# Splitting the gated retention output where it is formed, and loading both parts straight into the operand tiles

## The chip, the cores and the metric

The kernel runs on one core of one Trainium2 chip. The metric is the device time of one execution in microseconds (us). All values are float32. Products are made to full accuracy out of three matmuls on "split" operands: a tile x is kept as a high part hi (x rounded to the shorter type fp32r) and a low part lo = x - hi, and a product w*x is formed as hi*hi + hi*lo + lo*hi. So every matmul operand has to be split once, by a cast on ScalarE (ACT) and a subtraction on VectorE (DVE). TensorE is PE here, GpSimd is POOL, and SP is the SyncE queue that issues most of the DMAs.

## The reference, cut to what matters

One layer of a streaming encoder on 1024 prompt tokens and 64 sample tokens (T = 1088 columns in the kernel), model width 1024. The part around the change:

```python
def merge_branches(ret_o, ret_g, swa_o, gate_a, gate_b, w_ret_out, w_swa_out, w_mix_out):
    B, S = ret_g.shape[:2]
    a = (rms_norm(ret_o).astype(ret_g.dtype).reshape(B, S, -1) * jax.nn.silu(ret_g)) @ w_ret_out
    b = swa_o.reshape(B, S, -1) @ w_swa_out
    return (jax.nn.sigmoid(gate_a) * a + jax.nn.sigmoid(gate_b) * b) @ w_mix_out
```

`ret_o` is the output of multi-scale retention, normalised per head; `ret_g`, `gate_a` and `gate_b` are column blocks of one projection of the normalised input; `swa_o` is the output of sliding-window attention. After this come cross attention to 256 memory tokens, a SwiGLU and a last norm.

## The kernel before, in words

Activations are kept transposed: 128 partitions of model dimension by T columns, so a 1024-wide activation is KT = 8 tiles. The work is staged:

- `project_phase` (to about 825 us): projections with Strassen's seven products on halves of 544 columns (`strassen`, `weight_ops`), with retention of the four heads in between. Its operands B11, B21, B22, T1 to T4 lie in two rings of SBUF tiles: `rings[0]` and `rings[1]`, eight slots each, a slot being [128, 2, T]. Retention's normalised output goes to DRAM as `d_ret`.
- The last three projections of that phase are the gates: `w_ga` (sigmoid), `w_rg` (silu) and `w_gb` (sigmoid), each in four pairs of 128 output rows, each pair in two halves of columns. `project` evacuates a result into a `stage` tile (DVE), multiplies it by the token norm (DVE), applies the activation (ACT), and for `w_rg` alone loads `other` (the tile of `d_ret`, four buffers), multiplies on POOL, and stores the product to `d_gate[0]`. Between them steps of `memory_phase` run (`w_mk`, half of `w_mv`).
- `mix_phase` (from about 825 us): sliding-window attention (`swa`), 34 half-steps of scores, softmax, transpose and weighting (`scores`, `turn`, `weigh`). Between the half-steps PE does pieces of other products, handed out by `filler`: first the other half of `w_mv`, in eight pieces ahead of the first transposes, and then `w_ret_out` on the gated retention output, in 48 half-pieces of 12 matmuls. `in_order` fixes the order of PE's work here.
- `filler` first brings the gated retention output back: `operands(c0, n)` loads, for each of eight tiles and one of three chunks of columns CH (384, 384, 320), a part of `d_gate[0]` into a small tile `ld()` (ten of them, cut out of two slots of ring 0, named swin in the profile), and splits it (`split`: ACT at L123, DVE at L124) into `rets`, the eight slots of ring 1 (named ret in the profile).
- `merge_swa` and the later phases follow; the change does not touch them.

All queues are static: a scheduler that simulates the program's time line orders each engine's instructions when the kernel is built. `tc.issue_after(x)` keeps an instruction from being ordered before x; `high_priority` puts it early. SP's DMAs are issued in that fixed order: an issue that has to wait for a buffer holds up all behind it. `unit_raw` loads a slab of weights into one of two `raw` buffers; `unit_parts` splits it into `wq` tiles.

Of the kernel before, what the change touches and what calls it, by code (L numbers as in the profile page):

```python
# [11 lines left out]
F32 = mybir.dt.float32  # L12
F32R = mybir.dt.float32r
# [6 lines left out]
P = 128  # L20
D = 1024
KT = D // P
SEQ = 1024
SMP = 64
T = SEQ + SMP
CH = ((0, 384), (384, 384), (768, 320))
# [83 lines left out]
class Kernel:  # L110
# [8 lines left out]
    def store(self, out, in_):  # L119
        self.nc.sync.dma_start(out, in_)  # L120
# [212 lines left out]
    def run(self):  # L333
        nc, tc, io = self.nc, self.tc, self.io
        with ExitStack() as ctx:
            cp = ctx.enter_context(tc.tile_pool(name="const", bufs=1, reuse_waits="tile"))
            self.np = ctx.enter_context(tc.tile_pool(name="norm", bufs=1, reuse_waits="tile"))
            dp = ctx.enter_context(tc.tile_pool(name="scratch", bufs=1, reuse_waits="tile", space=DRAM))

            self.ident = cp.tile([P, P], F32, name="ident")  # L340
            self.ones = cp.tile([P, P], F32, name="ones")
            self.gains = cp.tile([P, 5, KT], F32, name="gains")
            self.load(self.gains, io["g_all"])
            nc.vector.memset(self.ones, 1.0)
            self.rstd = cp.tile([P, T], F32, name="rstd")

            self.root = cp.tile([P, len(CH), 3], F32, name="root")
            self.rtok = cp.tile([P, 9], F32, name="rtok")
            nc.vector.memset(self.rtok, 1.0)
            self.mtok = cp.tile([P, 2], F32, name="mtok")  # L350
            self.tab = cp.tile([P, 2, H, 3], F32, name="tab")
            self.tok = cp.tile([P, 3, H, 9], F32, name="tok")
            self.sinks = cp.tile([P, NPAIR], F32, name="sinks")

            self.d_mk = dp.tile([H, P, 2, NMEM], F32, name="d_mk")
            self.d_mv = dp.tile([H, P, 2, NMEM], F32, name="d_mv")
            self.d_ret = dp.tile([KT, P, T], F32, name="d_ret")
            self.d_swa = dp.tile([KT, P, T], F32, name="d_swa")
            self.d_gate = [dp.tile([KT, P, T], F32, name=f"d_gate{i}") for i in range(3)]
            self.d_mix = dp.tile([KT, P, T], F32, name="d_mix")  # L360
            self.d_h = [dp.tile([KT, P, T], F32, name=f"d_h{i}") for i in range(2)]
            self.d_op = dp.tile([len(OPS), FT // 2, P, HALF], F32, name="d_op")
            self.d_rb = dp.tile([16, 64 * 256], F32, name="d_rb")

            self.d_qkv = dp.tile([3, KT, P, T], F32, name="d_qkv")
            self.d_skv = dp.tile([2, P, T], F32, name="d_skv")
            self.d_sq = dp.tile([NPAIR // 2, P, 17, 2, 64], F32, name="d_sq")

            with ExitStack() as sctx:
                self.rings = [Ring(sctx.enter_context(tc.tile_pool(name=f"ring{i}", bufs=1, reuse_waits="tile", side="right")))  # L370
                              for i in range(2)]
                self.mem = sctx.enter_context(ExitStack())
                with self.weights(5):
                    self.project_phase()
                with self.weights(6):
                    with self.plain_psum():
                        self.mix_phase()
                        self.mem.close()
                        self.cross_phase()
                    rp = sctx.enter_context(tc.tile_pool(name="rf", bufs=1, reuse_waits="tile", side="right"))  # L380
                    self.rstd_f = rp.tile([P, T], F32, name="rstd_f")
                    self.temp = sctx.enter_context(ExitStack())
                    self.new_b12(self.temp, side="right")
                    self.cross_out_phase()
                    self.ffn_phase()
# [153 lines left out]
    def project_phase(self):  # L539
        nc, tc, io = self.nc, self.tc, self.io  # L540
        with ExitStack() as ctx:
# [9 lines left out]
            half = lambda t: slice(t * HALF, (t + 1) * HALF)  # L551
# [11 lines left out]
            def project(w, put, act=None, other=None):  # L563
                def emit(i, t, ps, sb):
                    o = taken(ps, sb)
                    (nc.vector if act is not None else nc.gpsimd).tensor_tensor(
                        out=o, in0=o, in1=self.rstd[:, half(t)], op=ALU.mult)
                    if act is not None:
                        nc.scalar.activation(o, o, act)
                    if other is not None:  # L570
                        r = op.tile([P, HALF], F32, tag="other", bufs=4, name="other")
                        self.load(r, other(i)[:, half(t)])
                        nc.gpsimd.tensor_tensor(out=o, in0=o, in1=r, op=ALU.mult)
                    put(i, t, o)
                cast = self.last_cast
                self.strassen(w, self.ops, emit)
                return cast
# [71 lines left out]
            steps = [0, 0, 0, 0, 1, 2, 2, 2, 3, 3, 2, 0]  # L649
            for idx, w, act in ((1, "w_ga", AF.Sigmoid), (0, "w_rg", AF.Silu), (2, "w_gb", AF.Sigmoid)):  # L650
                for m in range(0, KT, 2):
                    store = nc.scalar.dma_start if idx else self.store
                    put = lambda i, t, o, idx=idx, m=m, store=store: store(self.d_gate[idx][m + i, :, half(t)], o)
                    other = None if idx else lambda i, m=m: self.d_ret[m + i]
                    with tc.issue_after(project(pair(w, m // 2), put, act, other)):
                        for i in range(steps.pop(0)):
                            if (idx, m, i) == (0, 6, 0):
                                with tc.issue_after(self.last_mm):
                                    next(memory)
                            else:  # L660
                                next(memory)
# [378 lines left out]
    def filler(self):  # L1040

        nc, tc, io = self.nc, self.tc, self.io
        if True:
            def ld():
                self.lds.append(self.lds.pop(0))
                return self.lds[-1]

            rets = self.ring_tiles(1, KT, "ret")

            def operands(c0, n):  # L1050
                after = self.loaded
                for k in range(KT):
                    a = ld()
                    with tc.issue_after(after):
                        ins = self.load(a[:, :n], self.d_gate[0][k, :, c0:c0 + n])
                    if c0 == 0:
                        self.operand_loaded = ins
                    self.split(a[:, :n], rets[k][:, 0, c0:c0 + n], rets[k][:, 1, c0:c0 + n])

            raws = [self.unit_raw(io["w_mv"][3, i], 4, 256) for i in range(2)]  # L1060
            operands(*CH[0])
            for h in range(2, H):
                us = self.first_units if h == 2 else [self.unit_parts(raw, 4, 256) for raw in raws]
                operands(*CH[h - 1])
                for t in range(2):
                    ps = self.dense_psum()
                    for k in range(KT):
                        x = self.ms[k][:, :, t * P:(t + 1) * P]
                        self.mm3(ps[:, :256], x[:, 0], x[:, 1], *us[k // 4][k % 4], k == 0, k == KT - 1)
                        if k == 3:  # L1070
                            yield
                    o = ld()[:, :256]
                    nc.scalar.mul(o, ps[:, :256], self.mtok[:, t:t + 1])
                    self.store(self.d_mv[h, :, t, :], o)
                    self.store(io["o_mv"][t * P:(t + 1) * P, h * 256:(h + 1) * 256], o)
                    yield
            for m in range(KT):
                u = self.unit(io["w_ret_out"][m], KT)
                for c0, n in CH:
                    g = ld()  # L1080
                    self.load(g[:, :n], self.d_gate[1][m, :, c0:c0 + n])
                    for ps in self.pieces(u, rets, c0, n):
                        if ps is None:
                            yield
                    nc.vector.tensor_tensor(out=g[:, :n], in0=ps, in1=g[:, :n], op=ALU.mult)
                    self.store(self.d_mix[m, :, c0:c0 + n], g[:, :n])
                    yield
# [512 lines left out]
```

## Time and profile before

| | us |
|---|---|
| median of 3 runs | 2273.01 (2269.17 to 2275.49) |
| the profiled execution | 2270.68 |
| its span, first to last instruction | 2268.9 |
| mean granted PE clock over the span | 0.983 |

The profile is of one execution. Each engine's busy time counts its instructions alone, not its waits; "PEld" is the weight load that overlaps the matmuls. A wait is given as the waiting instruction, then the one that released it. In the DMA issues, "KB" is the size of one transfer and the last number the median us from issue to landing. DMA share is the mean busy share of the core's 16 DMA engines.

### The profile page before, as it was taken

The page shows a single profiled execution, that of the slowest core. Times are in us where ns is not written, and L with a number is a line of the kernel's source. Part 1 is how long each engine was busy: PE and PEld are TensorE (multiplying, and loading weights), DVE is VectorE, ACT ScalarE, POOL GpSimd, SP SyncE. Part 2 cuts the span into 40 slices and gives each one's busy share as a digit, 9 for nine tenths or more (in the row PEclk, how much of TensorE's full clock was granted, in tenths as well). Part 3 has the DMA queues.
Part 4 walks back from the last instruction along what each step waited for, and adds up shares of the span by engine and source line. Part 5 has one row for each costly group of instructions (what it writes and reads, how often), then busy time and mean ns, then how long its engine had stood idle before and what let it go on. Part 6 is the DMA issues. An engine that isn't in the chain of part 4 may idle for free.

```text
span 2268.9 us, 41687 instructions
## 1 busy us (share of the span) xinstructions
PE 2187.2 (96%) x16382; PEld 2121.9 (94%) x16382; DVE 1594.4 (70%) x2656; ACT 895.8 (39%) x1921; POOL 692.5 (31%) x466
## 2 busy tenths in 40 slices
PE   7999999999999989999999999999999999999996
PEld 7999998999999987778999998999999999999996
DVE  8986877666687658875455555676676776878596
ACT  7333333345444355553133333333222222344344
POOL 1441533332243112220000000014555555434471
PEclk9999999999999999999999999999999999999997
DMA  5644445443454475326443112422333332475223
GB/s 191 190 139 132 131 146 140 132 134 117 150 164 154 146 241 174 113 70 196 141 151 106 56 48 67 133 81 88 116 128 103 101 118 90 143 266 194 79 90 107
DMA packets 186406, 298.64 MB, mean 132 GB/s; under 512 B 40514, under 2 KB 111074, under 8 KB 186210
## 3 DMA queue, kind: packets, MB, share of 16 engines
q1 hardware_dynamic: 181602, 287.06, 39.6%
q10 hardware_dynamic: 4608, 8.91, 1.1%
q8 instruction: 129, 2.11, 0.4%
q14 instruction: 67, 0.55, 0.1%
HBM read 204.75 MB, written 91.16 MB: 130 GB/s over the span
## 4 chain that ended last, share of the span: by engine, by line
PE 77%; DVE 12%; DMA 5%; issue 3%; ACT 2%; POOL 1%; SPq 0%; DVEq 0%; ACTq 0%; POOLq 0%
PE pq L205 14%; PE pq L208 14%; PE pq L206 14%; PE pd L149 7%; PE pd L150 7%; PE pd L151 7%; DVE wq L124 2%; PE pout L987 2%; PE pp L971 1%; PE pss L929 1%; DMA cs<-c_rope 1%; DVE B L124 1%; DMA hl<-d_op 1%; DVE T L124 1%; DVE stage L560 1%
## 5 line engine op out<-in xcount | busy, mean ns | idle before, releaser
L123 ACT CAST wq<-raw 128x512 fp32r<-128x512 f32 (+1 forms) x509 | 310.2, 614 | 567.6 <-PE pq L208 275.9
L124 DVE TENSOR_TENSOR wq<-raw,wq 128x512 fp32r<-128x512 f32 (+1 forms) x509 | 449.6, 887 | 119.7 <-ACT wq L123 117.5
L205 PE MATMUL pq<-T,wq 128*128 128x272 f32 x1832 | 502.5, 292 | 2.9 <-DVE T L124 2.4
L206 PE MATMUL pq<-T,wq 128*128 128x272 f32 x1832 | 498.8, 289 | 0.0
L205 PE MATMUL pq<-B,wq 128*128 128x272 f32 x1592 | 439.2, 293 | 11.3 <-ACT wq L123 10.1
L206 PE MATMUL pq<-B,wq 128*128 128x272 f32 x1592 | 437.2, 291 | 7.7 <-DVE B L124 7.6
L208 PE MATMUL pq<-T,wq 128*128 128x272 f32 x1832 | 383.7, 289 | 0.6 <-DVE wq L124 0.6
L183 POOL TENSOR_TENSOR raw<-raw 128x512 f32<-128x512 f32 (+1 forms) x59 | 83.1, 1408 | 892.4 <-DVE wq L124 663.1
L205 PEld LDWEIGHTS pq<-T,wq 128*128 128x128 f32 x1832 | 346.7, 189 | 3.8 <-ACT wq L123 3.2
L206 PEld LDWEIGHTS pq<-T,wq 128*128 128x128 f32 x1832 | 349.9, 191 | 0.3 <-issue 0.3
L208 PE MATMUL pq<-B,wq 128*128 128x272 f32 x1592 | 334.3, 290 | 0.0
L206 PEld LDWEIGHTS pq<-B,wq 128*128 128x128 f32 x1592 | 305.9, 192 | 10.1 <-DVE B L124 9.7
L205 PEld LDWEIGHTS pq<-B,wq 128*128 128x128 f32 x1592 | 303.1, 191 | 11.9 <-ACT wq L123 10.1
L208 PEld LDWEIGHTS pq<-T,wq 128*128 128x128 f32 x1832 | 286.3, 189 | 1.9 <-DVE wq L124 1.2
L208 PEld LDWEIGHTS pq<-B,wq 128*128 128x128 f32 x1592 | 250.4, 190 | 0.5 <-issue 0.3
L252 DVE TENSOR_TENSOR u<-pq,u 128x544 f32<-128x544 f32 x177 | 127.5, 720 | 120.5 <-PE pq L208 119.8
L186 POOL TENSOR_TENSOR raw<-raw 128x512 f32<-128x512 f32 (+1 forms) x59 | 83.7, 1419 | 122.7 <-DVE wq L124 115.1
L957 POOL TENSOR_TENSOR t<-t,den 128x768 f32<-128x768 f32 (+2 forms) x34 | 47.9, 1408 | 173.5 <-DVE den L955 87.7
L560 DVE TENSOR_TENSOR stage<-pq,u 128x544 f32<-128x544 f32 x112 | 80.2, 716 | 28.5 <-PE pq L208 28.4
L184 POOL TENSOR_TENSOR raw<-raw 128x512 f32<-128x512 f32 (+1 forms) x59 | 87.1, 1476 | 3.7
L189 POOL TENSOR_TENSOR raw<-raw 128x512 f32<-128x512 f32 (+1 forms) x59 | 83.7, 1419 | 4.5
L1434 POOL TENSOR_TENSOR y<-u,y 128x544 f32<-128x544 f32 x38 | 62.5, 1652 | 73.7 <-DVE y L1432 51.5
(356 smaller groups left out, 4685.5 us busy)
## 6 DMA issues: line engine op xcount, KB each, us to landing
hl<-d_op SPq DMA_DIRECT2D x85, 272.0 KB, 4.4
d_qkv<-stage SPq DMA_DIRECT2D x44, 272.0 KB, 4.4
d_op<-stage SPq DMA_DIRECT2D x44, 272.0 KB, 2.2
d_op<-ht SPq DMA_DIRECT2D x44, 272.0 KB, 3.2
raw<-w_gate SPq DMA_DIRECT2D x22, 512.0 KB, 3.4
raw<-w_up SPq DMA_DIRECT2D x22, 512.0 KB, 4.8
cs<-c_rope SPq DMA_DIRECT2D x16, 544.0 KB, 4.3
d_gate<-stage ACTq DMA_DIRECT2D x32, 272.0 KB, 2.4
```

The source lines that it names most:

```text
L123: self.last_cast = self.nc.scalar.copy(hi, src).ins
L124: self.nc.vector.tensor_tensor(out=lo, in0=src, in1=hi.bitcast(F32), op=ALU.subtract)
L149: mm(ps, wh, xh, start=start, stop=False)
L150: mm(ps, wh, xl, start=False, stop=False)
L151: self.last_mm = mm(ps, wl, xh, start=False, stop=stop).ins
L184: tt(out=a21, in0=a21, in1=a22, op=add)
L186: tt(out=a11, in0=a22, in1=a11, op=sub)
L205: mm(ps[:, c, :HC], w[:, 0, ks], x[:, 0, cs], start=start, stop=False)
L206: mm(ps[:, c, :HC], w[:, 0, ks], x[:, 1, cs], start=False, stop=False)
L208: self.last_mm = mm(ps[:, c, :HC], w[:, 1, ks], x[:, 0, c * HC:(c + 1) * HC], start=False, stop=stop).ins
L252: add = lambda out, a, b: nc.vector.tensor_tensor(out=out, in0=a, in1=b, op=ALU.add)
L560: nc.vector.tensor_tensor(out=o, in0=ps, in1=sb, op=ALU.add)
```

## The change

The product of `w_rg`'s projection and `d_ret` is split at once: the cast writes the high part over the `other` tile, the subtraction leaves the low part in the `stage` tile. Both go to DRAM, into a new tensor `d_gret` [KT, 128, 2, T], by two stores in place of one. `operands` in `filler` has no splits and no small tiles any more: it loads both parts of a chunk with one DMA into the slot of ring 1, in the order 0, 1, 4, 5, 6, 7, 2, 3, the first chunk not before the memory weights loaded ahead (`after`), the later ones not before the first chunk's last load.

```diff
@@ -356,7 +356,8 @@
             self.d_mv = dp.tile([H, P, 2, NMEM], F32, name="d_mv")
             self.d_ret = dp.tile([KT, P, T], F32, name="d_ret")
             self.d_swa = dp.tile([KT, P, T], F32, name="d_swa")
-            self.d_gate = [dp.tile([KT, P, T], F32, name=f"d_gate{i}") for i in range(3)]
+            self.d_gate = [None] + [dp.tile([KT, P, T], F32, name=f"d_gate{i}") for i in (1, 2)]
+            self.d_gret = dp.tile([KT, P, 2, T], F32, name="d_gret")
             self.d_mix = dp.tile([KT, P, T], F32, name="d_mix")
             self.d_h = [dp.tile([KT, P, T], F32, name=f"d_h{i}") for i in range(2)]
             self.d_op = dp.tile([len(OPS), FT // 2, P, HALF], F32, name="d_op")
@@ -571,7 +572,12 @@
                         r = op.tile([P, HALF], F32, tag="other", bufs=4, name="other")
                         self.load(r, other(i)[:, half(t)])
                         nc.gpsimd.tensor_tensor(out=o, in0=o, in1=r, op=ALU.mult)
-                    put(i, t, o)
+                        hi, lo = r.bitcast(F32R), o.bitcast(F32R)
+                        self.split(o, hi, lo)
+                        put(i, t, 0, r)
+                        put(i, t, 1, o)
+                    else:
+                        put(i, t, o)
                 cast = self.last_cast
                 self.strassen(w, self.ops, emit)
                 return cast
@@ -649,8 +655,10 @@
             steps = [0, 0, 0, 0, 1, 2, 2, 2, 3, 3, 2, 0]
             for idx, w, act in ((1, "w_ga", AF.Sigmoid), (0, "w_rg", AF.Silu), (2, "w_gb", AF.Sigmoid)):
                 for m in range(0, KT, 2):
-                    store = nc.scalar.dma_start if idx else self.store
-                    put = lambda i, t, o, idx=idx, m=m, store=store: store(self.d_gate[idx][m + i, :, half(t)], o)
+                    if idx:
+                        put = lambda i, t, o, idx=idx, m=m: nc.scalar.dma_start(self.d_gate[idx][m + i, :, half(t)], o)
+                    else:
+                        put = lambda i, t, part, o, m=m: self.store(self.d_gret[m + i, :, part, half(t)], o)
                     other = None if idx else lambda i, m=m: self.d_ret[m + i]
                     with tc.issue_after(project(pair(w, m // 2), put, act, other)):
                         for i in range(steps.pop(0)):
@@ -1047,21 +1055,18 @@
 
             rets = self.ring_tiles(1, KT, "ret")
 
-            def operands(c0, n):
-                after = self.loaded
-                for k in range(KT):
-                    a = ld()
+            def operands(c0, n, after):
+                for k in (0, 1, 4, 5, 6, 7, 2, 3):
                     with tc.issue_after(after):
-                        ins = self.load(a[:, :n], self.d_gate[0][k, :, c0:c0 + n])
-                    if c0 == 0:
-                        self.operand_loaded = ins
-                    self.split(a[:, :n], rets[k][:, 0, c0:c0 + n], rets[k][:, 1, c0:c0 + n])
-
+                        ins = self.load(rets[k].bitcast(F32)[:, :, c0:c0 + n], self.d_gret[k, :, :, c0:c0 + n])
+                return ins
+
+            after = self.loaded
             raws = [self.unit_raw(io["w_mv"][3, i], 4, 256) for i in range(2)]
-            operands(*CH[0])
+            self.operand_loaded = operands(*CH[0], after)
             for h in range(2, H):
                 us = self.first_units if h == 2 else [self.unit_parts(raw, 4, 256) for raw in raws]
-                operands(*CH[h - 1])
+                operands(*CH[h - 1], self.operand_loaded)
                 for t in range(2):
                     ps = self.dense_psum()
                     for k in range(KT):
```

## Prediction

> **What bounds the kernel now.** First the page: its span, the busy engines, and the chain of work that ended last, by engine.
>
> ```profile
> span 2268.9 us, 41687 instructions
> ...
> PE 2187.2 (96%) x16382; PEld 2121.9 (94%) x16382; DVE 1594.4 (70%) x2656; ACT 895.8 (39%) x1921; POOL 692.5 (31%) x466
> ...
> PE 77%; DVE 12%; DMA 5%; issue 3%; ACT 2%; POOL 1%; SPq 0%; DVEq 0%; ACTq 0%; POOLq 0%
> ```
>
> The matmul engine is busy 96% of the span and carries 77% of the chain. So DVE and ACT instructions that vanish pay nothing in themselves; only idle or slow-clock time of PE can be won or lost. Next, the two places that the change touches, in windows: the stage of the gate projections (620 to 720) and the seam where the projections end and attention begins. The columns after the width are busy us of PE, PEld, DVE, ACT and POOL, then granted PE clock, DMA share and GB/s.
>
> ```profile
> 620.00:720.00 100.00, 100.00 (x803) 100.00 (x802) 81.52 (x106) 45.85 (x80) 49.84 (x33) 1.00 0.47 156
> ...
> 815.40:829.20 13.80, 10.79 (x85) 10.23 (x84) 7.00 (x11) 3.93 (x7) 0.00 (x0) 0.97 0.44 122
> 829.20:845.40 16.20, 11.67 (x83) 11.04 (x82) 11.60 (x31) 11.68 (x36) 1.38 (x2) 0.82 0.96 352
> ...
> 835.88:850.78 14.90, 10.37 (x70) 9.44 (x69) 12.98 (x31) 13.12 (x41) 1.38 (x2) 0.77 1.06 378
> 850.78:868.23 17.45, 15.34 (x85) 12.21 (x85) 13.57 (x36) 11.77 (x41) 2.46 (x2) 0.80 0.93 304
> 868.23:872.44 4.21, 4.21 (x32) 3.35 (x31) 3.92 (x10) 2.88 (x14) 1.47 (x1) 1.00 0.25 90
> 868.23:960.00 91.77, 91.77 (x656) 71.36 (x655) 74.68 (x162) 49.39 (x191) 24.95 (x17) 1.00 0.36 112
> ```
>
> In the gate stage PE never idles. In the seam it does, its clock falls to about 0.8, and the DMA engines are full (share 0.96 at 352 GB/s). From 868.23 PE is busy without a gap at full clock: what the seam loses or gains before that is kept to the end. Who made PE wait in the seam (us in total, times, longest):
>
> ```profile
> PE pd L149 <- ACT swin L1073: 3.5, 1, 3.5
> PE pout L987 <- ACT pT L974: 2.1, 1, 2.1
> ```
>
> These two, the longest of the seam, are waits for ACT, whose queue holds splits that the change moves away. Last, the order of time, SP's DMA issues with what they feed:
>
> ```profile
> 814.07 1.29 SPq L117 DMA_DIRECT2D swin<-d_rb  x2
> 829.22 0.33 SPq L117 DMA_DIRECT2D raw<-w_mv  x1
> ...
> 830.80 6.29 SPq L117 DMA_DIRECT2D swin<-d_gate  x8
> ...
> 838.88 0.85 SPq L117 DMA_DIRECT2D swin<-d_gate  x2
> 839.98 0.86 SPq L117 DMA_DIRECT2D raw<-w_ret_out  x2
> ...
> 845.42 1.67 ACT L123 CAST wq<-raw 128x512 fp32r<-128x512 f32 x3
> ...
> 850.78 0.44 PE L149 MATMUL pd<-ret,wq 128*128 128x384 f32 x1
> ...
> 868.23 0.42 PE L149 MATMUL pd<-ret,wq 128*128 128x384 f32 x1
> ```
>
> SP stands from 815.4 to 829.2, as w_mv needs a free weight buffer. Then ten gate loads go out, w_ret_out's first two slabs behind them; w_ret_out is cast at 845.42 and PE's first matmul on the retention operand comes at 850.78. PE takes that product in half-pieces between attention steps: the fourth begins at 868.23.
>
> **The change part by part: splits that go.**
>
> ```profile
> L124 DVE TENSOR_TENSOR ret<-swin,ret 128x384 fp32r<-128x384 f32 (+1 forms) x24 | 12.2, 543 | 2.9 <-ACT ret L123 2.9
> ...
> L123 ACT CAST ret<-swin 128x384 fp32r<-128x384 f32 (+1 forms) x24 | 10.5, 490 | 1.8 <-DMA swin<-d_gate 1.8
> ```
>
> 24 casts (10.5 us of ACT) and 24 subtractions (12.2 us of DVE) leave the seam. The 3.5 us wait goes with them: its releaser is one PSUM copy queued behind seven of these casts. That is a gain only if nothing else is late then; something is (below).
>
> **Splits that come, in the gate stage.** Sixteen tiles of 128x544 get a cast and a subtraction.
>
> ```profile
> L124 DVE TENSOR_TENSOR wq<-raw,wq 128x512 fp32r<-128x512 f32 x32 | 35.2, 1105 | 11.6 <-ACT wq L123 11.4
> ...
> L573 POOL TENSOR_TENSOR stage<-stage,other 128x544 f32<-128x544 f32 x16 | 24.9, 1560 | 31.0 <-ACT stage L569 31.0
> ```
>
> The moved splits had 363 columns in the mean (16 of 384, 8 of 320); scaled to 544, a cast is 0.73 us and a subtraction 0.81. ACT: 16 x 0.73 = 11.7 us on top of 45.85 in 100; room enough. DVE: 16 x 0.81 = 13.0 us where it runs undisturbed; in this stage a weight split of 512 columns takes 1.105 us, or 1.17 for 544, so up to 18.8. DVE then stands at 94.5 to 100.3 of 100 us. That just fits under PE's 100, which hides it; where that cover ends, each us beyond is PE's. The added wait: DVE's subtraction waits for ACT's cast, that for POOL's product (1.56 us), and behind the subtraction in DVE's queue stand weight splits and PSUM evacuations that PE needs. In the built kernel's order one to three other DVE instructions stand between. One product is 24 matmuls, about 3 us by the 803 in 100 us, and there are three PSUM buffers, so a DVE instruction late by 1 to 3 us reaches no matmul. I take 0, with 0 to +5 as bounds, the upper being a third of a us for each tile.
>
> [...]
>
> Stores: 32 instead of 16 in this stage, at DMA share 0.47 and on SP; behind them on SP stand the slabs of w_rg and w_gb, a few issues of some 0.4 us later, and in the trace no matmul of 600 to 730 waits for anything. 0.
>
> **The loads, which decide.** What is issued in the seam, with its size and the median us to landing:
>
> ```profile
> swin<-d_gate SPq DMA_DIRECT2D x23, 192.0 KB, 4.3
> ...
> swin<-d_gate SPq DMA_DIRECT2D x11, 160.0 KB, 5.2
> ...
> d_mv<-swin SPq DMA_DIRECT2D x4, 128.0 KB, 4.0
> ```
>
> A gate load carries two parts now: 384 KB or 320 KB in place of 192 and 160. SP's order in the built changed kernel is: bias, five gate loads, w_mv, one gate load, queries, w_mv, two gate loads, keys and values, eight gate loads, four stores of 128 KB (d_mv and o_mv), eight gate loads of 320 KB, and only then w_ret_out. Before, ten gate loads stood ahead of it. The first five now go out in the pause of 815 to 829, where DMA stood at 0.44: free. After 829.2 there stand ahead of w_ret_out 3 + 8 loads of 384, 8 of 320 and four stores of 128: 4224 + 2560 + 512 = 7296 KB, against 10 x 192 = 1920 KB. The difference, 5376 KB or 5.5 MB, takes 15.6 us at 352 GB/s. So w_ret_out's cast goes from 845.42 to 861.1, and with 0.6 us for it PE's first retention matmul from 850.78 to about 861.8: 11.0 us later. PE has nothing else: its order is fixed, and the mem-value matmuls and two score steps ahead of it are done near 850 even if they lose some us to the later w_mv.
>
> [...]
>
> What is won back: from 850.78 to 868.23 three half-pieces with their attention steps took 17.45 us, with a 2.1 us wait for ACT and clock 0.80. At full clock a step is 4.21 us, three 12.6. After a pause of some 10 us PE starts at a low clock again; the old stretch lost (1 - 0.80) x 17.45 = 3.5 us that way, and I take 3. So 15.6 in place of 17.45: 1.8 won. Sum: 11.0 - 1.8 + 0 = +9.2 us, rounded to +9.
>
> The profiled execution took 2270.68 us (span 2268.9 and 1.8 around it), 2.3 below the median 2273.01; I add the 9 to each: span about 2278, median 2282. Bounds: at the row that averages the whole crowded stretch after, 304 GB/s, the delay is 18.1 us (+2.5); at the fullest row, 378 GB/s, it is 14.6 (-1), and if the low clock costs nothing, another -3. With the +5 of the gate stage that is +5 to +16.
>
> **Rivals.** First, not slower: the loads do not delay. If the DMA engines have spare rate in the seam, or more than five loads leave before 829, w_ret_out is there by 847, and PE, without the 3.5 us wait, starts the product at 847.3, does three steps in 12.6 + 2 us and reaches 868.23's work at about 862: 6 us faster, median 2267. It decides where the loads ahead of w_ret_out are done by 846. For it: 24 splits gone from two engines that PE waited for. Against it: the 0.96 share. A weaker form, half the delay, gives about 0 to +5.
>
> Second, DVE becomes the bound of the gate stage. If every subtraction waits out a whole product of POOL, 16 x (0.81 + 1.56) = 37.9 us; DVE at 119 of 100 us would cost up to 19 us beside the seam's 9, median 2290 to 2300. It decides where one subtraction costs over (100 - 81.5) / 16 = 1.16 us. For it: 1.17 us is as close as can be. Against: DVE's idle time is there already net of such waits, and ACT separates POOL's product from its subtraction.
>
> Third, the change does not do what it says: the splits could have stayed in the seam beside the new ones. The built order has no split of a retention tile left there, so 0 chance.
>
> **How the numbers follow.** Forecast (w_ret_out behind the loads, +5 to +13): 0.62. Half the delay (0 to +5): 0.16. DVE-bound gate stage (+13 to +28): 0.10. Not slower (-8 to 0): 0.12. The predicted time is the first's, 2282. The range leaves out the last rival's faster half and most of the second rival: 2269 to 2290. About 0.3%, 6.8 us, is what a measurement of this kernel tells from no change. Slower by more than that: three quarters of the forecast case, 0.47, and the DVE case, together 0.57. Faster by more: two thirds of the first rival, 0.08, since it stands right at that mark. Within: the rest, 0.35.
>
> **What would show it.** Right: the first matmul reading ret near 862, PE idle some 10 us before it with w_ret_out's cast as releaser, itself released by a DMA; DMA share near 1 from 829 to 860; the fourth half-piece near 877; no PE wait in 620 to 730. Wrong: w_ret_out landing before 850, a wait of PE on DVE in the gate stage, or PE gaps after 880 that were not there.

## The result, and the profile after

The changed kernel takes 2288.69 us in the median of 6 runs (2284.99 to 2292.1), the kernel before 2269.38 (2268.37 to 2275.49, 6 runs beside it). The ratio is 1.0077 with a 95% interval of 1.0063 to 1.0092: slower by 0.8%, 19.3 us between the medians. The prediction was 2282, 9 us slower. The profiled execution of the changed kernel took 2284.99 us, its fastest, so the traces show a somewhat smaller difference than the medians: 14.2 us between the spans.

The page of the changed kernel, with span, busy engines and the chain's shares:

```profile
span 2283.1 us, 41668 instructions
...
PE 2182.6 (96%) x16382; PEld 2116.5 (93%) x16382; DVE 1596.6 (70%) x2648; ACT 895.8 (39%) x1913; POOL 693.5 (30%) x466
...
PE 75%; DVE 12%; DMA 6%; ACT 3%; issue 2%; POOL 1%; SPq 0%; DVEq 0%; ACTq 0%; POOLq 0%
```

ACT is as busy as before (895.8 us) and DVE by 2.2 us more: the splits have moved, none has gone. What PE waited for in the changed kernel, first from 600 to 740 (the gate stage, where it waited for nothing before), then from 810 to 900 (the seam):

```profile
PE pq L205 <- ACT u L255: 2.5, 2, 1.8
PE pq L205 <- DVE stage L561: 0.7, 2, 0.4
PE pq L205 <- DVE u L252: 0.6, 1, 0.6
```

```profile
PE pd L149 <- ACT wq L123: 20.1, 3, 14.7
PE pss L937 <- DVE stage L561: 0.8, 1, 0.8
```

So there are two losses. To size them, three moments are read in each trace: **A**, the start of the last copy of retention's output (tile ret_t); **S**, the first score matmul, where the seam begins; **R**, the first matmul on the retention operand. And **E**, the last one. In the changed kernel these are 591.3, 832.62, 872.4 and 1070.6. Three rows of the changed kernel show where they are read. The view of the tile ret_t (min/median/max ns, then first and last start; L820 was L812 before) gives A, the timeline of PE gives S, the view of the tile ret gives R and E (first and last start of each line's matmuls; weight loads left out):

```profile
L820 DVE COPY ret_t<-pb x20: 280/681/695, 135.8 to 591.3; 128x512 f32<-128x512 f32 x16, 128x128 f32<-128x128 f32 x4
```

```profile
832.62 0.66 PE L937 MATMUL pss<-swin,swin 64*128 64x64 f32 x8 [0.81 <-DVE stage L561]
```

```profile
L149 PE MATMUL pd<-ret,wq x192: 307/336/686, 872.4 to 1070.3; 128*128 128x384 f32 x128, 128*128 128x320 f32 x64
...
L151 PE MATMUL pd<-ret,wq x192: 305/336/608, 873.2 to 1070.6; 128*128 128x384 f32 x128, 128*128 128x320 f32 x64
```

Before, A was 590.8, S 825.40, R 850.78 and E 1050.0. The stage, A to S, went from 234.6 to 241.3 us (+6.7: the waits of 3.8 us above, and 2.9 that PE was busy longer, 236.70 in place of 233.78 us, with the same matmuls), the seam, S to R, from 25.4 to 39.8 (+14.4), and R to E from 199.2 to 198.2. That makes +20.6 at E. Some 4 us come back right after it. The stretch of 110 us from E on, in the kernel before, then in the changed one (width, busy us of PE, PEld, DVE, ACT, POOL; clock, DMA share, GB/s):

```profile
1050.00:1160.00 110.00, 107.99 (x646) 107.67 (x645) 58.85 (x110) 32.05 (x61) 0.00 (x0) 0.98 0.53 165
```

```profile
1070.60:1180.60 110.00, 110.00 (x670) 110.00 (x669) 60.12 (x112) 32.35 (x63) 0.00 (x0) 1.00 0.55 167
```

Before, PE waited 2.0 us there for a split of the attention output, and its clock fell after it (0.57 from 1057 to 1061); in the changed kernel this wait is absent, and `w_swa_out` ends 16.6 us later than before in place of 20.6.

### The profile page after: what moved, and what is told of

The parts are those of the page before. It is cut to its first block, busy times and chain, and to the rows that moved or that the text cites. A ratio compares the mean times of both kernels' runs of the same rounds, so it can differ in the third digit from the quotient of the medians.

```text
span 2283.1 us, 41668 instructions
## 1 busy us (share of the span) xinstructions
PE 2182.6 (96%) x16382; PEld 2116.5 (93%) x16382; DVE 1596.6 (70%) x2648; ACT 895.8 (39%) x1913; POOL 693.5 (30%) x466
## 4 chain that ended last, share of the span: by engine, by line
PE 75%; DVE 12%; DMA 6%; ACT 3%; issue 2%; POOL 1%; SPq 0%; DVEq 0%; ACTq 0%; POOLq 0%
PE pq L205 14%; PE pq L208 14%; PE pq L206 14%; PE pd L149 7%; PE pd L151 7%; PE pd L150 7%; DVE wq L124 2%; PE pout L995 1%; PE pp L979 1%; DMA cs<-c_rope 1%; DMA hl<-d_op 1%; PE pss L937 1%; DVE T L124 1%; DVE B L124 1%; DVE stage L561 1%
```

## The experiments

Twelve kernels were run, each against runs of the kernel before on the same chip (its medians there: 2268.64 to 2270.66). This table sets the stages of their profiles, of one execution each, and their times side by side (us; ratio to before, 95% interval). The five kernels without a split in the stage agree within 0.4 us in A to S:

| kernel | A to S | S to R | R to E | median | ratio |
|---|---|---|---|---|---|
| before | 234.6 | 25.4 | 199.2 | | |
| changed | 241.3 | 39.8 | 198.2 | 2288.69 | 1.0077 (1.0063 to 1.0092) |
| 1 stage only | 240.1 | 25.2 | 197.3 | 2274.15 | 1.0024 (1.0010 to 1.0037) |
| 2 loads only | 234.7 | 40.7 | 198.3 | 2283.09 | 1.0062 (1.0047 to 1.0077) |
| 3 loads only, one part | 234.8 | 33.2 | 197.0 | 2273.00 | 1.0022 (1.0009 to 1.0036) |
| 4 gate tiles late | 240.6 | 39.8 | 198.5 | 2287.65 | 1.0081 (1.0068 to 1.0094) |
| 5 weights first | 241.4 | 28.6 | 196.6 | 2275.39 | 1.0019 (1.0008 to 1.0031) |
| 6 store queue | 240.5 | 36.4 | 198.4 | 2281.53 | 1.0050 (1.0035 to 1.0065) |
| 7 weights first, store queue | 240.6 | 24.9 | 196.5 | 2271.15 | 1.0008 (0.9997 to 1.0020) |
| 8 before, store queue | 235.0 | 25.6 | 200.3 | 2271.90 | 1.0017 (1.0007 to 1.0026) |
| 9 no subtraction | 237.8 | 42.3 | 198.4 | 2285.55 | 1.0070 (1.0055 to 1.0085) |
| 10 no cast | 240.1 | 43.2 | 198.6 | 2288.37 | 1.0082 (1.0067 to 1.0097) |
| 11 neither | 234.6 | 41.7 | 198.2 | 2283.67 | 1.0062 (1.0049 to 1.0074) |
| 12 subtraction on POOL | 240.3 | 23.8 | 198.7 | 2272.41 | 1.0018 (1.0008 to 1.0028) |

### Each half of the change alone

**1, the stage only.** From the changed kernel, with the old `operands`:

```diff
+                    a = ld()
+                        ins = self.load(a[:, :n], self.d_gret[k, :, 0, c0:c0 + n])
+                    self.split(a[:, :n], rets[k][:, 0, c0:c0 + n], rets[k][:, 1, c0:c0 + n])
```

> The gate stage of the changed kernel (cast, subtraction and two stores for each of 16 tiles) with the seam of the kernel before: the seam loads the stored high part alone into the small tiles and splits it again, so the low part of the product is left out of the result. Theory (two costs that add): the stage costs its own 6 to 7 us, the projections end near 832 in place of 825.4, and the time is 6 us above the kernel before, about 2276. Rival (the late end of the projections in the one profile is chance, and all of the 19 us is made in the seam): within 2 us of the kernel before, 2268 to 2272. Rival (the stage's cost is taken up by slack of the seam, which waits for DMA anyway): projections end near 832, but the first matmul on the retention operand still near 851, and the time within 2 us of before.

Measured: 2274.15, the ratio 1.0024, 5.5 us by it; the stage 240.1, the seam 25.2 as before. The theory's 6 us holds, and both rivals fall.

**2, the loads only.** From the kernel before, with the changed `operands`:

```diff
+                        ins = self.load(rets[k].bitcast(F32)[:, :, c0:c0 + n],
+                            self.d_gate[0][k, :, c0:c0 + n].unsqueeze(1).broadcast_to([P, 2, n]))
```

> The gate stage of the kernel before with the seam of the changed kernel: no splits in the seam, each load fills both halves of the operand tile, here twice from the same unsplit product, so the bytes and the order of the issues are the changed kernel's and the values of the low part are wrong. Theory (two costs that add): the projections end near 825 and the first matmul on the retention operand comes 12 to 14 us later than before, near 864; time 8 to 12 us above before, 2278 to 2282. Rival (all of it is made in the seam): 17 to 20 us above before, 2287 to 2290. Rival (the seam by itself gains, as the splits are gone, and only a late gate stage makes it lose): 0 to 6 us below before.

Measured: 2283.09, the ratio 1.0062, 14.1 us by it. R is 865.4, as the theory has it; the time is above its 8 to 12, and below the rival's 17 to 20. The two halves add up: 5.5 + 14.1 = 19.6, against 17.5 by the ratio and 19.3 by the medians of the whole change.

**3, half the bytes.** As 2, but `rets[k].bitcast(F32)[:, 0, ...]` is loaded alone, and the matmuls read it twice.

> The gate stage of the kernel before; the seam has no splits and loads the unsplit product straight into the high half of the operand tile, one part alone, so that the bytes are those of the kernel before; the matmuls read that half in place of the low one, so the values of the low part are wrong. Order and waits of SP's queue are those of the run with both parts (2283.09, +14.1 us against before). Theory (order and waits make most of the loss, bytes some): half the bytes, 4.4 MB or 12.5 us at 352 GB/s of the seam's transfers, are gone, the first matmul on the retention operand comes 8 to 12 us earlier than the 865.4 of that run, and the time is 2 to 6 us above before, 2271 to 2275: removing the splits does not pay even without the bytes, while the loads stand ahead of the weights. Rival (all of the loss is bytes, and the splits' removal is worth the 3.5 us wait of PE): 2 to 6 us below before, 2263 to 2267. Rival (the wait for the gate store and the loads' late start make all of it): 10 to 14 us above before.

Measured: 2273.00, 3.5 us above the 2269.53 beside it (ratio 1.0022), R at 858.4, 7 us earlier than in 2 where 8 to 12 were expected. The theory's range for the time holds. Even with the old bytes and no splits, the seam is 7.8 us longer than before: bytes are half of its 15.3, and the rest is not bytes: the splits are gone too, so it lies in how the loads stand in the queue.

### Where the seam's time goes

SP's issues in the changed kernel (start, us, counts; a group's us run from its first issue to its last, waits included):

```profile
822.79 0.32 SPq L117 DMA_DIRECT2D swin<-d_gate  x1
823.20 0.86 SPq L117 DMA_DIRECT2D raw<-w_mv  x2
824.11 1.30 SPq L117 DMA_DIRECT2D swin<-d_rb  x2
825.46 12.33 SPq L117 DMA_DIRECT2D ret<-d_gret  x5
837.89 0.54 SPq L117 DMA_DIRECT2D raw<-w_mv  x1
...
845.40 9.33 SPq L117 DMA_DIRECT2D ret<-d_gret  x8
...
858.43 6.64 SPq L117 DMA_DIRECT2D ret<-d_gret  x8
865.17 1.02 SPq L117 DMA_DIRECT2D raw<-w_ret_out  x2
```

All 24 operand loads stand ahead of w_ret_out, as predicted. But the first five do not go out in the pause before S: they take 12.33 us, from 825.46 on. SP's waits from 805 to 870 name two releasers that hardly counted before (1.5 us and 2.7 us there):

```profile
SPq L117 <- DMA d_gate<-stage: 9.2, 2, 8.2
SPq L117 <- PE pq L208: 8.6, 1, 8.6
```

The second is the load of a tile of the mixing gate at 822.79: the small tiles have become free for it, so it is ordered early, and it then waits for PE to leave its slot. **4 takes this wait away**:

```diff
-                    self.load(g[:, :n], self.d_gate[1][m, :, c0:c0 + n])
+                    with tc.issue_after(self.operand_loaded):
+                        self.load(g[:, :n], self.d_gate[1][m, :, c0:c0 + n])
```

> The changed kernel with one edit: the loads of the mixing gate's tiles for the retention product may not be issued before the first chunk's last operand load. In the changed kernel six of them go out early, and the sixth holds the SP queue for 8.6 us, until PE frees its slot, with the memory weights, the bias table and the operand loads behind it. Theory (that wait is a part of the seam's cost): the bias table goes out before 818 in place of 824, five operand loads use the pause before the end of the projections, and the time is 4 to 7 us below the changed kernel, 2281 to 2285. Rival (the DMA engines are the only limit of the seam, and all the bytes have to pass ahead of the first weights anyway): within 2 us of the changed kernel, 2287 to 2290.

Measured: 2287.65, the seam 39.8 long, no different. The theory fell, and the trace of 4 shows why: w_mv and the bias table go out earlier, at 816.15 and 822.22, but the operand loads do not. SP's timeline of 4 and its longest wait:

```profile
822.22 1.29 SPq L117 DMA_DIRECT2D swin<-d_rb  x2
825.46 12.89 SPq L117 DMA_DIRECT2D ret<-d_gret  x5
```

```profile
SPq L117 <- DMA d_gate<-stage: 11.9, 3, 5.6
```

The first releaser was the one that mattered. No operand load needs a tile that these stores of w_gb's results (L659, on ACT's queue) use. The built program explains it: in it, each issue on SP or ACT counts on one of eight completion semaphores (DMAHW0 to DMAHW7) in turn, and first waits until the transfer that used its semaphore last has landed. In the program's order, the first three operand loads and the last three of these stores, each with what its issue waits for:

```
SP  ret<-d_gret 128x2x384 [DMAHW2]
SP  ret<-d_gret 128x2x384 [DMAHW3]
SP  ret<-d_gret 128x2x384 [DMAHW4]
ACT d_gate<-stage 128x544 [DMAHW3, Activation]
ACT d_gate<-stage 128x544 [DMAHW4, Activation]
ACT d_gate<-stage 128x544 [DMAHW0, Activation]
```

In the trace of the changed kernel these three stores leave ACT at 828.65, 831.03 and 834.04, when their results exist. The second operand load, on semaphore 3, is issued at 834.37, after a wait of 8.2 us; the third, on 4, at 835.96. The loads are tied to the end of the projections, though neither data nor slot ties them. **6 takes w_gb's stores to GpSimd's queue**, in addition to 4. They are sixteen, not the eight that its expectation names, and in the built program they then count on semaphores of their own:

```diff
-put = lambda i, t, o, idx=idx, m=m: nc.scalar.dma_start(
+put = lambda i, t, o, idx=idx, m=m: (nc.gpsimd if idx == 2 else nc.scalar).dma_start(
```

> The kernel with the mixing gate's loads held back and, as the one further edit, the eight last gate results (w_gb) stored from GpSimd's queue in place of ScalarE's. In the kernels run so far the second operand load waited 5.6 to 8.2 us in SP's queue for one of those stores to land, on a completion semaphore that eight transfers share in turn, while the DMA engines stood idle for some us; the memory weights stand behind it. Theory (that wait is the seam's second loss beside the order): the operand loads go out one behind the other from 826, the memory weights before 834, and the time is 3 to 6 us below the kernel that only holds the gate back (2287.65), 2281 to 2285. Rival (the full DMA engines make up for the pause, as they did for the earlier bias table): within 2 us of it, 2286 to 2290.

Measured: 2281.53, 6.1 us below 4 (by the two ratios 7), the seam 36.4, 3.4 us shorter. The timeline of SP in 6:

```profile
819.62 1.29 SPq L117 DMA_DIRECT2D swin<-d_rb  x2
820.96 3.90 SPq L117 DMA_DIRECT2D ret<-d_gret  x6
834.21 0.33 SPq L117 DMA_DIRECT2D raw<-w_mv  x1
...
859.80 0.54 SPq L117 DMA_DIRECT2D raw<-w_ret_out  x1
```

Six loads are out by 824.9, 6 us before S (830.95). The theory holds in the time; of it the seam shows 3.4 us. The remainder is not accounted for: these are two profiles of one execution each, and the one of 6 stands 2.5 us earlier at A already. What the expectation says of idle DMA engines is too strong: in the changed kernel the share was 0.45 and 0.13 from 820 to 824, while the mixing gate's load blocked SP, but about 1 from 826 to 834.

**5 puts the weights first**, with 4's idea kept:

```diff
-                operands(*CH[h - 1], self.operand_loaded)
...
                 u = self.unit(io["w_ret_out"][m], KT)
+                if m == 0:
+                    for ch in CH[1:]:
+                        operands(*ch, self.loaded)
```

> The kernel with the mixing gate's loads held back, and in addition the operand loads of the second and third chunk not issued before the first slab of the retention output weights, so that 16 loads (5.6 MB, 16 us at 352 GB/s) stand behind that slab in place of ahead of it. Theory (the seam is lost to bytes ahead of the weights): the first matmul on the retention operand comes near 857, 15 us earlier than in the changed kernel, and the time is 12 to 16 us below the changed kernel, 2273 to 2277, with the gate stage's 6 to 7 us left over against before. Rival (the bytes are needed anyway, and what the weights gain the later chunks lose): the first matmul comes early, but PE then waits for the second and third chunk, and the time is 3 to 7 us below the changed kernel, no better than holding back the mixing gate alone.

Measured: 2275.39, 13.3 us below the changed kernel. The seam shrinks by 11.2 us to 28.6; R is 863.1, 9.3 us earlier than in the changed kernel, not 15. PE does not wait for the later chunks (R to E 196.6), so the rival falls.

**7 joins both**, with the mixing gate's loads behind w_ret_out's slab too:

> The first slab of the retention output weights ahead of the second and third chunk of operand loads and of the mixing gate's loads, and the last gate results stored from GpSimd's queue: every repair of the seam together, with the gate stage as changed. Theory (the seam's cost is order and waits, not bytes): the first matmul on the retention operand comes 3 to 6 us earlier than in the run with the weights first (2275.39), and the time is 2270 to 2273, even with the kernel before, the stage's 5.5 us being made up by the seam without splits. Rival (what was to be had by order is had already): 2274 to 2277, PE waiting for the second and third chunk instead.

Measured: 2271.15, ratio 1.0008 (0.9997 to 1.0020): no difference from before that these runs can tell. The weights leave at 846.54, ahead of the sixteen later loads, and PE's wait for the weights' casts from 810 to 900 falls from 20.1 us in all to 5.6. SP's timeline of 7 and the first of PE's waits:

```profile
846.54 0.33 SPq L117 DMA_DIRECT2D raw<-w_ret_out  x1
846.93 13.66 SPq L117 DMA_DIRECT2D ret<-d_gret  x16
```

```profile
PE pd L149 <- ACT wq L123: 5.6, 3, 3.5
```

The seam is back at 24.9 us with both parts loaded, so repairing order and waits gives back the whole 14.4 us: no byte less is moved, but 5632 KB of it after the weights, where no wait of PE for it shows. Whether the bytes still cost something that the missing splits pay for is not shown; no run loads one part in this order.

**8, the control**, the store queue alone on the kernel before:

> The kernel before with the eight last gate results (w_gb) stored from GpSimd's queue in place of ScalarE's: the control for the runs with that edit. Theory (in the kernel before SP stands in the pause for the memory weights' buffer anyway, and waited only 1.5 us for such a store): within 2 us of before, 2267 to 2271. Rival (the edit is worth the same everywhere): 5 to 7 us below before, 2262 to 2264.

Measured: 2271.90, ratio 1.0017 (1.0007 to 1.0026): if anything slower, by 1.6 to 6 us, where 2 either way was expected. In that kernel, where no operand load waits long for those stores, the edit is worth nothing.

### Where the stage's time goes

One incident first, the longest wait of PE in the changed kernel's stage. ACT's instructions, in order:

```profile
693.15 0.65 ACT L123 CAST other<-stage 128x544 fp32r<-128x544 f32 x1 [1.76 <-POOL stage L574]
693.82 1.28 ACT L290 ACT_TABLE_LOAD   x1
...
695.22 0.64 ACT L123 CAST other<-stage 128x544 fp32r<-128x544 f32 x1
695.88 1.28 ACT L570 ACT_TABLE_LOAD   x1
...
698.24 0.60 ACT L255 COPY u<-pq 128x544 f32<-128x544 f32 x1
```

A moved cast waits 1.76 us for POOL's product, and the PSUM copy for which PE waits 1.85 us (until 698.90) stands behind two of these casts and two table loads. It suggests that casts that wait for POOL are the cause. 9, 10 and 11 take the parts of the split away:

```diff
-                        self.split(o, hi, lo)
+  9:                    self.last_cast = nc.scalar.copy(hi, o).ins
+ 10:                    nc.vector.tensor_tensor(out=lo, in0=o, in1=r, op=ALU.subtract)
+ 11:                    (nothing; the two stores stay)
```

> The changed kernel without the 16 subtractions of the gate stage: the cast and both stores stay, the second store carries the unsplit product, so the low part is wrong. From the last retention copy to the first attention scores the kernel before took 234.6 us, the three kernels with the splits in the stage 240 to 241. Theory (casts that wait for POOL's product hold up ACT's queue, and with it a PSUM copy that PE needs): the length stays at 239 to 241 and the time within 2 us of the changed kernel, 2286 to 2290. Rival (the subtraction's two SBUF operands load VectorE and slow POOL's product, which went from 1.37 to 1.81 us in the median): the product goes back to 1.37 us, the length to 236 or less, and the time is 4 to 7 us below the changed kernel, 2281 to 2285.

> The changed kernel without the 16 casts of the gate stage: the subtraction takes the loaded tile itself in place of the cast's result, so that it waits for POOL's product alone, and both stores stay; both parts are wrong. Theory (casts that wait for POOL hold up ACT): the waits of PE for ACT's PSUM copy (2.5 us) go, the length from the last retention copy to the first scores falls to 237 or less, and the time is 4 to 6 us below the changed kernel, 2282 to 2285. Rival (subtractions against POOL): the length stays at 240 to 241, POOL's product at 1.8 us, and the time within 2 us of the changed kernel.

> The changed kernel without the 16 casts and without the 16 subtractions of the gate stage; the two stores for each tile stay (the loaded tile and the unsplit product), so both parts are wrong. From the last retention copy to the first attention scores it took 234.6 us before, 241.3 in the changed kernel, 240.1 without the casts, 237.8 without the subtractions. Theory (ACT and VectorE are both full in short stretches, and each part of the split costs PE about 3 us there): the length falls to 234 to 235.5, the stage waits of PE are gone, and the time is 5 to 7 us below the changed kernel, 2281 to 2284. Rival (the 3 us that are left without the subtractions are the 16 additional stores, behind which the weight slabs stand in SP's queue): 237 to 238.5, and 2284 to 2287.

Measured, A to S: 237.8 without subtractions, 240.1 without casts, 234.6 with neither, the length of before; the times are 2285.55, 2288.37 and 2283.67. So the stores are free, and the split's two instructions are all of the 6 us. The theory of the casts fell: without them the length stays. Its rival has the direction right, but not the size, since the casts alone still cost 3.2 us, and not the reason, since POOL's product stayed at 1.80 us. The two do not add up (3.2 with casts alone, 5.5 with subtractions alone, 6.7 with both): each alone finds a queue in which something for PE stands behind it. The 5.5 us without casts can be read: PE waits 3.9 us more than before (2.0 for ACT's PSUM copies, 0.6 for DVE's evacuations, 0.8 and 0.5 for a weight split's cast and subtraction), and is busy 1.6 us longer (235.40 from A to S). The longest of these waits, 1.21 us until 699.19, can be followed back in the trace of 10. Its rows, of POOL, DVE, DVE, ACT and ACT:

```profile
692.48 3.13 POOL L574 TENSOR_TENSOR stage<-stage,other 128x544 f32<-128x544 f32 x2
694.33 1.87 DVE L576 TENSOR_TENSOR stage<-stage,other 128x544 fp32r<-128x544 f32 x1 [0.55 <-POOL stage L574]
696.72 0.71 DVE L567 TENSOR_TENSOR stage<-stage,rstd 128x544 f32<-128x544 f32 x1
697.46 0.66 ACT L570 ACTIVATE stage<-stage 128x544 f32<-128x544 f32 x1 [2.08 <-DVE stage L567]
698.53 0.60 ACT L255 COPY u<-pq 128x544 f32<-128x544 f32 x1
```

A subtraction begins while POOL's second product runs, and takes 1.87 us where most take 0.71. The multiplication by the token norm (L567) stands behind it, ACT's activation waits 2.08 us for that, and the PSUM copy that PE needs stands behind the activation. So a subtraction on DVE reaches PE through ACT's queue too.

**12** is 7 with the subtraction on POOL, to relieve DVE:

```diff
-                        self.split(o, hi, lo)
+                        self.last_cast = nc.scalar.copy(hi, o).ins
+                        nc.gpsimd.tensor_tensor(out=lo, in0=o, in1=r, op=ALU.subtract)
```

> The best order of the seam so far (weights first, last gate results from GpSimd's queue: 2271.15) with the gate stage's 16 subtractions on GpSimd in place of VectorE, whose stretches of 690 to 697 and 712 to 720 were full. Theory (half of the stage's 6 us are the subtractions' time on VectorE): VectorE is relieved, POOL has room (49.8 of 100 us and 16 times 1.4 to 1.8 more), and the time is 1 to 4 us below that run, 2267 to 2270, not slower than before. Rival (POOL's subtractions delay its weight sums, which the casts and so the matmuls wait for, or slow VectorE's two-operand instructions): 2272 to 2278.

Measured: 2272.41, ratio 1.0018 (1.0008 to 1.0028) against 1.0008 (0.9997 to 1.0020) for 7: no gain, the stage still 240.3 long. The theory fell: DVE lost its 15.8 us of subtractions, but was busy only 3.5 us less from A to S than in 7 (174.92 in place of 178.45), as its other instructions took longer. The two intervals overlap, so whether it is worse than 7 stays open. No version here beat the kernel before; 7 cannot be told from it.

## Why the prediction was right, and where it was wrong

**The direction and the main term were right.** The seam was said to lose because all operand loads stand ahead of w_ret_out, 11.0 us to the first retention matmul; it lost 14.4, and 5 and 7 show that this order is the cause. From the changed kernel's windows, before S, and from S to R:

```profile
815.00:832.62 17.62, 16.80 (x135) 16.58 (x134) 7.88 (x13) 2.60 (x4) 0.00 (x0) 1.00 0.80 225
832.62:872.38 39.76, 19.12 (x125) 17.69 (x126) 11.79 (x34) 14.38 (x45) 2.78 (x3) 0.72 1.01 352
```

The full stretch ran at the 352 GB/s that the sum used, share 1.01 (before: 0.87 at 314).

**The step "the first five now go out in the pause: free" failed.** The built order put them early, but order is not time: SP stood 8.6 us behind a gate tile's load and 8.2 us on a shared semaphore, and one load left before 834. The waits of an issue were not read, only its place in the queue. Run 6 gives back 3.4 us of the seam, as much as 14.4 exceeds 11.0; between single executions, that the two agree to a tenth is partly chance. That the doubled bytes by themselves were the cost was half right: 3 gets back 7.5 of 15.3 us by halving them, 7 gets back all without.

**What is won back** was 1.8 us for the three half-pieces after R. The fourth half-piece began at 887.77 in place of 868.23, 19.5 later with R 21.6 later: 2.1. Right. The wait of 2.0 us in the next phase, gone with its slow clock, was not foreseen; it gave back 4.

**"I take 0" for the gate stage failed**, and its upper bound of 5 too: 6.7. The instructions are no longer than estimated: a cast takes 0.65 us for 0.73, and the subtractions 15.8 us in all, between the 13.0 and the 18.8 of the estimate.

```profile
L124 DVE TENSOR_TENSOR stage<-stage,other 128x544 fp32r<-128x544 f32 x16 | 15.8, 994 | 1.1 <-ACT other L123 1.1
```

The step that failed is that DVE's mean load "just fits under PE's 100", so that an instruction late by 1 to 3 us reaches no matmul. In short stretches DVE has no room (columns as above):

```profile
690.00:697.00 7.00, 7.00 (x57) 6.83 (x55) 6.86 (x11) 5.19 (x8) 4.90 (x3) 1.00 0.16 57
697.00:700.00 3.00, 1.15 (x8) 1.10 (x8) 1.72 (x4) 2.56 (x6) 1.34 (x1) 0.95 0.98 308
700.00:704.00 4.00, 4.00 (x22) 4.00 (x22) 3.40 (x6) 1.61 (x3) 0.69 (x1) 0.61 0.96 288
704.00:708.00 4.00, 4.00 (x34) 4.00 (x33) 3.83 (x6) 1.80 (x3) 0.68 (x1) 1.00 0.76 269
...
712.00:720.00 8.00, 8.00 (x69) 8.00 (x69) 8.00 (x9) 3.89 (x7) 6.60 (x5) 1.00 0.61 209
```

DVE is busy 6.86 of 7 us and then 8.00 of 8, while its mean from 620 to 720 is 88.4 of 100. A full stretch alone does not make PE wait, though. In the kernel before there was one too, and PE waited for nothing:

```profile
660.00:670.00 10.00, 10.00 (x82) 10.00 (x81) 9.75 (x11) 2.92 (x6) 6.92 (x4) 1.00 0.25 78
```

In the chain of 10 above, what counts is that something PE needs stands behind the late instruction. The longest waits were for ACT, whose mean of 50 looked safe.

**The rivals.** "Not slower" is out: w_ret_out leaves at 865.17, not by 847. "DVE becomes the bound" came half true, at a third of its price and through ACT's queue as well. What its sum supposes, that a subtraction waits for an instruction of POOL, does show when each instruction is looked at. In the changed kernel eleven of the 16 subtractions took 0.70 to 0.73 us. The other five, of 1.26 to 1.82, are those that began while a POOL instruction ran, and each ended 0.58 to 0.59 us behind the end of that one. Such a pair:

```profile
716.00 1.82 DVE L124 TENSOR_TENSOR stage<-stage,other 128x544 fp32r<-128x544 f32 x1
```

```profile
715.57 1.66 POOL L183 TENSOR_TENSOR raw<-raw 128x512 f32<-128x512 f32 x1 [1.32 <-issue]
```

That makes some 4.4 us of waiting in all (15.8 against 16 x 0.71), where the rival's price was 16 x 1.56, 25 us. The 1.105 us of a weight split that the prediction counts with are a mean of two kinds: in that stage of the kernel before, one takes 0.67 to 0.70 us when no POOL instruction runs beside it, and up to 1.78 when one does. POOL waits in its turn: its products took 1.34 to 1.37 us, or 1.72 to 1.86 when they began during a DVE instruction with two inputs in SBUF. Ten of 16 were long in the changed kernel, seven before. So the medians of 10 and 9, below, are no measure of these waits: seven and nine were long there.

```profile
L574 POOL TENSOR_TENSOR stage<-stage,other x16: 1338/1372/1856, 632.8 to 719.6; 128x544 f32<-128x544 f32 x16
```

```profile
L574 POOL TENSOR_TENSOR stage<-stage,other x16: 1332/1800/1844, 632.3 to 716.0; 128x544 f32<-128x544 f32 x16
```

In sum, the forecast of +9.2 stands against 20.6 at E. The 11.4 between them are 0.5 from before A, 6.7 from the stage, 3.4 from the pause, and 0.8 from R to E, where 1.0 was won in place of 1.8. The unforeseen 4 us and smaller gains later leave 14.2 in the spans. That 2288.69 lies inside the range of 2269 to 2290 is partly luck. The forecast's own bounds were +5 to +16, and the medians side by side differ by 19.3; the range was laid around 2273.01, and the runs beside the changed kernel put the kernel before at 2269.38.

## What to carry to other kernels

A transfer that is ordered early leaves early only if nothing ahead of it in the queue waits (8.6 us in the changed kernel), and its own completion semaphore is free (8.2 us there): read an issue's waits, not its place. When loads take over the work of instructions, put what PE needs first ahead of what it needs later; with the doubled bytes behind the weights the seam was as short as before (24.9 us against 25.4). And judge the room for added instructions by what stands behind them in the queue, on every engine whose queue also empties PSUM, and by what runs on POOL beside them (a subtraction of 0.71 us took up to 1.82); a mean over a stage shows neither.

## What the runs showed of the hardware

PE's clock fell after a short wait: in the changed kernel a wait of 1.85 us was followed by 4 us at 0.61, with 22 matmuls in place of 34 (rows above), so by the 12 that are missing it cost an estimated 1.4 us more than its own length. But waits of up to 1.9 us left the clock at 1.00 in runs 1 and 5 (every window from 660 to 740), and so did 1.03 us in 9 (697 to 704). The length of a wait alone does not decide it; what does is not shown here.

Subtractions of DVE with two inputs in SBUF waited out POOL's instructions (in the changed kernel 0.70 to 0.73 us alone, up to 1.82 beside one), and POOL's products waited out DVE's (1.34 to 1.37 us, or 1.72 to 1.86). In run 10 a PSUM copy on ACT was held up by this at second hand, through the order of two queues, and PE waited 1.21 us for it.

Moving sixteen stores to another queue (6 against 4) shortened a seam by 3.4 us, though the DMA engines stayed full (share 0.98 from S to R in 6). In the built program it took the stores out of the rotation of semaphores on which SP's issues wait; SP waited 11.9 us for such stores in 4 from 805 to 870, and in 6 its waits name none.
